# Prompt attention of a hybrid decoder: the causal mask as a GpSimd select on the weights, and plain copies of the turned weights on ScalarE or VectorE

## The chip, the cores and the metric

The kernel runs on one core of one Trainium2 chip. Its time is the device time of one execution in microseconds (us); the median over the runs is compared. The engines are called as in the profile: PE (TensorE matmul), PEld (TensorE weight load), DVE (VectorE), ACT (ScalarE), POOL (GpSimd), SP (SyncE, which issues DMAs).

## What is computed

One mixer layer of a decoder for a prompt of 2048 tokens and for 8 samples of 4 tokens: a projection into head groups (convolution, pooling, stick-breaking attention, cross-attention), gates, an output projection and norms. The change is in the stick-breaking attention of the prompt, 8 heads of 64:

```python
def sb_block(q, k, v, bias, q_pos, k_pos):
    z = (jnp.einsum('nqhd,nkhd->nhqk', q, k).astype(jnp.float32) * (SB_HEAD_DIM ** -0.5)
         + bias.astype(jnp.float32)[None, :, None, None])
    mask = (k_pos[None, :] < q_pos[:, None])[None, None]
    log_beta = jax.nn.log_sigmoid(z)
    log_1m = jnp.where(mask, jax.nn.log_sigmoid(-z), 0.0)
    rc = lax.cumsum(log_1m, axis=3, reverse=True)
    a = jnp.exp(jnp.where(mask, log_beta + rc - log_1m, -jnp.inf))
    return jnp.einsum('nhqk,nkhd->nqhd', a.astype(v.dtype), v)
```

For each query the weight of key k is beta(k), the sigmoid of the score, times the product of (1 - beta) over all later keys before the query. Keys from the query's own position on have weight zero.

## The kernel before

The program has three stages in a row: the projection with the sample group's attention beside it (to about 1476 us of the profile), the prompt's attention (to about 1946 us), and the output projection. All operations are handed to a scheduler that sets the order on ACT, DVE, POOL and SP; on PE the order is the one in which the code issues them (`manual_schedule`, L145). Every engine works through its own queue in order.

`sb_prompt` (L1289) goes over 16 blocks: head pair `hp` 0 to 3, and in each the query block `qb` 0 to 3 of 512 queries. In a block the key chunks `kc` of 512 keys run from `qb` down to 0; the chunk `kc == qb` is the diagonal one (`dg`). Each chunk has four steps, one for head `hh` 0 or 1 and `q2` 0 or 2, a pair of query tiles of 128 rows. So a head pair has 40 steps, 16 of them diagonal, and the stage has 160.

One step, in `score`:
- PE computes the scores S of two query tiles against `w` keys (512, or 256 in the diagonal chunk's first pair; L1267, two buffers).
- ACT makes the gates from S: `gam` = 1 - beta (L1271, three buffers in turn) and the weight factor `be` = beta (L1272).
- `rest`, which is issued two steps later, has DVE scan `gam` backwards into the running product E (L1337 in a diagonal chunk, L1340 in others, one scan per tile; the scan's second operand ZM is a mask column in PSUM that starts the diagonal products), and POOL multiply `be` by E in place (L1349, one product per tile) and keep E's last column in `cr` as the next chunk's start (L1345).

Six steps after a chunk's first step, `turn` takes its 128-key squares: for key tile `r` and head `hh` PE transposes the up to four squares into one PSUM tile AT (L1360, two buffers), which is taken out to `at` in SBUF (four buffers). In a diagonal chunk the squares before tile r are skipped, so the tile has 512, 384, 256 or 128 columns, and the exit is a product with the triangle `tri` on DVE (L1364): it clears the entries of keys that do not come before the query. In other chunks it is a copy on ACT (L1366). Two steps after that `values` multiplies `at` with the values into the accumulator `av` (L1376, a single buffer), and at a block's end DVE multiplies `av` with the gate into `sbo` (L1381).

The first two steps (head pair 0, block 0, `q2` 0) are computed ahead by `sb_early` (L1274) into a buffer named `early`, while the projection still runs. `zm` and `tri` are built on POOL at the start of the stage (L1293 to L1300); ACT copies `zm` into PSUM as ZM (L1297).

Between the steps a side task is stepped: the end of the sample group's attention (nS, nE, nyn, nys: L1076 to L1137), sums of output weights on POOL (`ws`, L1587), splits of weights (ACT L1623, POOL L1628) and of activations (ACT L1717, POOL L1728), and the start of the convolution's tail (cs, cm, L1447 to L1459).

## Time and profile before

| | |
|---|---|
| median of 3 runs | 2351.18 us |
| the three runs | 2357.12, 2351.18, 2350.86 us |
| span of the profiled execution | 2357.7 us |
| DVE, ACT, POOL busy over the span | 1705.4, 1115.4, 1299.0 us |
| the stage with the prompt's attention | about 1476 to 1946 us |

The profile is of one execution, whose span is 6.5 us above the median of the timed runs; for its own time only this span is given. A row of a group or a tile reads: line, engine, operation, output <- inputs, shape and count, then busy time and mean, or minimum, median and maximum in ns. A row of the timeline starts with the start time and the length in us, and has the idle time of the engine ahead of it, and what ended that, in square brackets. "PE AT L1360 <- DVE at L1364" in the waits view reads: on PE, the instruction of line 1360 that writes AT waited for the one of line 1364 on DVE that writes `at`.

### The profile page before, as it was taken

How to read it: one execution, taken by the hardware profiler on the slowest of the kernel's cores; microseconds unless marked ns; L12 is line 12 of the kernel's file. 1: busy time of each engine (PE TensorE's matmuls, PEld its weight loads, DVE VectorE, ACT ScalarE, POOL GpSimd, SP SyncE). 2: the span in 40 equal slices, each digit the busy share in tenths (PEclk: the TensorE clock that was granted, in tenths of full speed). 3: DMA queues.
4: the chain of work that ended last, by engine and by line, in shares of the span. 5: the costliest groups of instructions: out<-in, count | busy, mean ns of one | idle time of the engine just before them, and what ended most of it. 6: DMA issues, size and time to landing. Idle time of an engine off the chain costs nothing. (4 is left out here: it accounts for less than half of the span.)

```text
span 2357.7 us, 42145 instructions
## 1 busy us (share of the span) xinstructions
PE 2270.5 (96%) x16000; PEld 1762.9 (75%) x16000; DVE 1705.4 (72%) x2372; ACT 1115.4 (47%) x1935; POOL 1299.0 (55%) x1347
## 2 busy tenths in 40 slices
PE   7999999999999999999999999899999999999997
PEld 7898888888888777777777777555555557788775
DVE  5342786969657673577787868988897966586997
ACT  5332342242442322224242324798989875453553
POOL 3554546555565546545546463688988854432333
PEclk9999999999999999999999999999999999999999
DMA  6689987878678899987877785656544207876764
GB/s 208 199 293 308 332 273 255 278 254 290 240 260 314 314 350 341 321 286 257 304 264 258 274 269 148 178 166 167 163 124 117 77 23 231 277 230 190 244 244 145
DMA packets 336868, 557.94 MB, mean 237 GB/s; under 512 B 27985, under 2 KB 212433, under 8 KB 320266
## 3 DMA queue, kind: packets, MB, share of 16 engines
q1 hardware_dynamic: 281290, 286.53, 39.3%
q0 software_dynamic: 55376, 268.72, 32.0%
q8 instruction: 126, 2.06, 0.3%
q14 instruction: 76, 0.62, 0.1%
HBM read 465.09 MB, written 90.68 MB: 236 GB/s over the span
## 5 line engine op out<-in xcount | busy, mean ns | idle before, releaser
L971 DVE STREAM_TRANSPOSE T<-kt 128x1024 f32<-128x1024 f32 x256 | 308.7, 1226 | 188.7 <-PE sSA L984 176.3
L938 POOL DMA_INDIRECT vt<-in_cache_v_dram,idv x256 | 253.2, 989 | 256.1 <-PE sO L1023 195.3
L623 DVE SCALAR_TENSOR_TENSOR cacc<-U,par,cacc 128x512 f32<-128x512 f32 x480 | 359.9, 750 | 11.0
L1349 POOL TENSOR_TENSOR be<-be,E 128x512 f32<-128x512 f32 (+3 forms) x316 | 300.3, 965 | 59.6 <-DVE E L1340 26.7
L1340 DVE TENSOR_TENSOR_SCAN E<-gam,cr,ZM 128x513 f32<-128x513 f32 x192 | 232.8, 1263 | 14.2 <-ACT gam L1271 10.8
L938 POOL DMA_INDIRECT kt<-in_cache_k_dram,idk x128 | 127.7, 998 | 196.4 <-DVE T L971 151.3
L1360 PEld LDWEIGHTS AT<-ident,be 128*128 128x128 f32 x1082 | 115.7, 141 | 130.0 <-ACT at L1366 48.3
L1993 PE MATMUL acc<-wohi,mh 128*128 128x512 f32 (+1 forms) x480 | 194.2, 405 | 1.2 <-ACT mh L1717 1.2
L1271 ACT ACTIVATE gam<-S,nbias_bc 128x1024 f32<-128x1024 f32 (+1 forms) x158 | 173.1, 1096 | 42.4 <-ACT be L1272 19.4
L1993 PE MATMUL acc<-wolo,mh 128*128 128x512 f32 (+1 forms) x480 | 190.4, 397 | 0.7 <-DVE wolo L1628 0.7
L1993 PE MATMUL acc<-wohi,ml 128*128 128x512 f32 x448 | 178.6, 399 | 8.0 <-DVE ml L1728 8.0
L1267 PE MATMUL S<-kT,Q 128*128 128x512 f32 (+1 forms) x632 | 173.6, 397 | 4.3 <-ACT be L1272 4.3
L1272 ACT ACTIVATE be<-S,bias_bc 128x1024 f32<-128x1024 f32 (+1 forms) x158 | 172.1, 1089 | 0.8 <-DMA gsd<-sg1sg 0.8
L1360 PE MATMUL AT<-ident,be 128*128 128x128 f32 x1082 | 157.0, 282 | 15.7 <-DVE at L1364 8.6
L1376 PE MATMUL av<-at,V 128*64 128x512 f32 (+3 forms) x640 | 151.9, 554 | 3.5 <-DVE sbo L1381 3.5
L984 PE MATMUL sSA<-T,W 128*32 128x128 f32 x4096 | 140.0, 276 | 2.8 <-DVE T L971 1.4
L984 PEld LDWEIGHTS sSA<-T,W 128*32 128x32 f32 x4096 | 105.3, 109 | 38.7 <-issue 31.9
L1728 DVE TENSOR_TENSOR ml<-mr,mh 128x512 fp32r<-128x512 f32 x108 | 93.2, 869 | 45.2 <-ACT mh L1717 43.5
L1023 PE MATMUL sO<-vt,saT 128*32 128x512 f32 x1024 | 122.4, 592 | 0.0
L1267 PEld LDWEIGHTS S<-kT,Q 128*128 128x128 f32 x632 | 104.3, 192 | 18.1 <-ACT be L1272 5.8
L1366 ACT COPY at<-AT 128x512 f32<-128x512 f32 x192 | 111.3, 680 | 12.2 <-PE AT L1360 12.2
L1337 DVE TENSOR_TENSOR_SCAN E<-gam,ZM 128x384 f32<-128x384 f32 (+1 forms) x124 | 94.3, 811 | 28.8 <-ACT gam L1271 21.9
(584 smaller groups left out, 6021.5 us busy)
## 6 DMA issues: line engine op xcount, KB each, us to landing
Q<-qd SPq DMA_DIRECT2D x64, 256.0 KB
mr<-mixd SPq DMA_DIRECT2D x32, 512.0 KB
mr<-mixd SPq DMA_DIRECT2D x48, 256.0 KB
xtp<-in_x_prompt_dram SPq DMA_DIRECT2D x16, 512.0 KB
kT<-kd SPq DMA_DIRECT2D x64, 128.0 KB
ws<-in_w_out_dram SPq DMA_DIRECT2D x16, 512.0 KB
wsd<-ws SPq DMA_DIRECT2D x16, 512.0 KB
msd<-mr SPq DMA_DIRECT2D x32, 256.0 KB
```

Of the source, the lines that this page charges most:

```text
L623: dve.scalar_tensor_tensor(out=ps, in0=U[:, a + k : a + k + H], scalar=wd[:, k : k + 1], in1=ps, op0=ALU.mult, op1=ALU.add)
L938: pool.indirect_dma_start(out=dst, out_offset=None, in_=rows, in_offset=bass.IndirectOffsetOnAxis(ap=idx, axis=0))
L971: S["turn"] = dve.transpose(T[:, 2 * hh : 2 * hh + 2].rearrange("p s j t -> p (s j t)"), kt[:, 2 * hh : 2 * hh + 2].rearrange("p s j d -> ...
L984: pe.matmul(sSs[n][32 * g : 32 * g + 32, P * ml : P * (ml + 1)], lhsT=W[:, jj, :], rhs=T[:, :, jj, :], start=i == 0, stop=i == 3, tile_pos ...
L1267: pe.matmul(S[:, j, :w], lhsT=Q[:, x, P * (q2 + j) : P * (q2 + j + 1)], rhs=kt[:, :w], start=x == 0, stop=x == 1)
L1271: act.activation(out=ga, in_=S[:, :, :w], func=AF.Sigmoid, bias=nbias_bc[:, h : h + 1], scale=-1.0)
L1272: act.activation(out=be, in_=S[:, :, :w], func=AF.Sigmoid, bias=bias_bc[:, h : h + 1])
L1340: dve.tensor_tensor_scan(out=E[:, j][:, ::-1], data0=g_[:, j][:, ::-1], data1=ZM[:, 0:1].to_broadcast([P, 513]), initial=carry[hh, q2][:, ...
L1349: newest.append(pool.tensor_tensor(out=be[:, j, :m], in0=be[:, j, :m], in1=E[:, j, 513 - w : 513 - w + m], op=ALU.mult).ins)
L1360: pe.transpose(ap_[:, P * qt : P * (qt + 1)], A[hp, qb, kc, hh, qt][:, P * r : P * (r + 1)], ident)
L1376: pe.matmul(av[64 * hh : 64 * hh + 64, c], lhsT=V[:, 4 * kc + r, 64 * hh : 64 * hh + 64], rhs=ats.pop((hp, qb, kc, r, hh))[:, c], start=dg ...
L1993: pe.matmul(o[:rows], lhsT=m[a][:, k, :rows], rhs=W[prod, 4 * h + k][w], start=not cont and h == k == n == 0, stop=h == 1 and k == 3 and n ...
```

## The change

The triangle `tri` is gone. A new function `sb_shut` clears, right behind the gates of a diagonal step, the two 128 x 128 squares of `be` that lie on the diagonal, with one select on POOL (`affine_select` over 2 x 128 columns, in place); POOL's products follow on the cleared tile. The early steps get the same, on the buffer `early`. So the turned squares need no mask, and each of the 320 exits from PSUM is a plain copy, on ACT or on DVE. Which one is decided when the program is built: `spent` adds up an estimate of the work that each of the two has got lately (gates and copies for ACT, scans and copies for DVE), the copy goes to the engine that would be done first, and an engine may fall at most SLACK = 3 us behind the other in that account.

```diff
--- before.py
+++ after.py
@@ -62,6 +62,7 @@
 MSTEP = 5
 KT = 2
 WR = 2
+SLACK = 3.0
 
 
 class Tasks:
@@ -1271,6 +1272,13 @@
         act.activation(out=ga, in_=S[:, :, :w], func=AF.Sigmoid, bias=nbias_bc[:, h : h + 1], scale=-1.0)
         act.activation(out=be, in_=S[:, :, :w], func=AF.Sigmoid, bias=bias_bc[:, h : h + 1])
 
+    def sb_shut(be, q2):
+
+        two = be[:, 0, P * q2 : P * q2 + P]
+        two = bass.AP(tensor=two.tensor, offset=two.offset, ap=[two.ap[0], [be.ap[1][0] + P, 2], [1, P]])
+        pool.affine_select(out=two, in_=two, compare_op=ALU.is_gt, fill=0.0, base=0, pattern=[[0, 2], [-1, P]],
+                           channel_multiplier=1)
+
     def sb_early(load, blk, sbr, bps, early):
 
         room = sbr.tile([P, 16, P], F32, tag="V", name="early", bufs=2).rearrange("p (n j b) c -> p n j (b c)", n=4, j=2)
@@ -1284,6 +1292,7 @@
             sb_scores(S, hh, 0, 2 * P, Q[hh], KT[0, hh, 0])
             early[hh] = room[:, 2 * hh], room[:, 2 * hh + 1]
             sb_gates(S, hh, 2 * P, *early[hh])
+            sb_shut(early[hh][1], 0)
             yield
 
     def sb_prompt(load, loaded, sb, bps, ops, zmp, early, values_of, flags, newest):
@@ -1295,10 +1304,6 @@
                            pattern=[[-1, P]], channel_multiplier=1)
         ZM = zmp.tile([P, 512], F32, name="ZM", bufs=1)
         act.copy(ZM, zm)
-        tri = sb.tile([P, 512], F32, name="tri", bufs=1)
-        pool.memset(tri, 1.0)
-        pool.affine_select(out=tri, in_=tri, compare_op=ALU.is_gt, fill=0.0, base=0, pattern=[[1, 512]],
-                           channel_multiplier=-1)
         gam = []
         for k in range(3):
             g = sb.tile([P, 2, 513], F32, name=f"gam{k}", bufs=1)
@@ -1307,6 +1312,12 @@
         blocks = [(hp, qb) for hp in range(4) for qb in range(4)]
         A, avs, ats = {}, {}, {}
         count = {"pair": 0}
+        spent = {act: 0.0, dve: 0.0}
+
+        def spend(eng, us):
+            spent[eng] += us
+            other = dve if eng is act else act
+            spent[other] = max(spent[other], spent[eng] - SLACK)
 
         def score(hp, qb, kc, hh, q2, Q, KT, carry):
 
@@ -1320,16 +1331,20 @@
             else:
                 S = ops.tile([P, 2, 512], F32, tag="S", name=f"S{nm}", bufs=2)
                 sb_scores(S, h, q2, w, Q[hh], KT[hp, hh, kc])
+                spend(act, 2 * (0.15 + 0.00166 * w))
                 be = sb.tile([P, 2, 512], F32, tag="be", name=f"be{nm}", bufs=10)
                 g_ = gam[count["pair"] % 3]
                 count["pair"] += 1
                 ga = g_[:, :, 512 - w : 512]
                 sb_gates(S, h, w, ga, be[:, :, :w])
+                if dg:
+                    sb_shut(be, q2)
             for j in range(2):
                 A[hp, qb, kc, hh, q2 + j] = be[:, j]
 
             def rest():
                 E = sb.tile([P, 2, 513], F32, tag="E", name=f"E{nm}", bufs=3)
+                spend(dve, 0.3 + 0.00204 * sum(ns))
                 for j, n in enumerate(ns):
                     if dg:
 
@@ -1360,10 +1375,14 @@
                 pe.transpose(ap_[:, P * qt : P * (qt + 1)], A[hp, qb, kc, hh, qt][:, P * r : P * (r + 1)], ident)
             at = sb.tile([P, 512], F32, tag="at", name=f"at{nm}", bufs=4)
             c = slice(P * q0, 512)
-            if dg:
-                dve.tensor_tensor(out=at[:, c], in0=ap_[:, c], in1=tri[:, : 512 - P * q0], op=ALU.mult)
+            n = 512 - P * q0
+            mine, its = 0.045 + 0.00083 * n, 0.13 + 0.00104 * n
+            if spent[act] + mine <= spent[dve] + its:
+                act.copy(at[:, c], ap_[:, c])
+                spend(act, mine)
             else:
-                act.copy(at[:, c], ap_[:, c])
+                dve.tensor_copy(at[:, c], ap_[:, c])
+                spend(dve, its)
             ats[hp, qb, kc, r, hh] = at
 
         def values(hp, qb, kc, r, V, gt):
```

The instructions on PE are the same, in the same order. On the others, as the program is built (the rows of now bear the changed kernel's line numbers, 1 to 19 higher; scans are listed as SCALAR_TENSOR_TENSOR):

ACT, at the start of the stage. S and gam are the scores and gates of the stage's first full step, ZM the mask column in PSUM. Before:

```order
L713 ACTIVATE sg1sg_1_14828<-z1sg_1_14794 128x512
L1271 ACTIVATE gam_14875<-S_0_0_0_2_14885,nbias_bc 128x2x512
L1272 ACTIVATE be_0_0_0_2_14890<-S_0_0_0_2_14885,bias_bc 128x1024
L1297 COPY ZM<-zm 128x512
L1271 ACTIVATE gam_14877<-S_0_0_1_2_14898,nbias_bc 128x2x512
L1272 ACTIVATE be_0_0_1_2_14903<-S_0_0_1_2_14898,bias_bc 128x1024
```

Now:

```order
L714 ACTIVATE sg1sg_1_14830<-z1sg_1_14795 128x512
L1272 ACTIVATE gam_14874<-S_0_0_0_2_14884,nbias_bc 128x2x512
L1306 COPY ZM<-zm 128x512
L1273 ACTIVATE be_0_0_0_2_14889<-S_0_0_0_2_14884,bias_bc 128x1024
L1272 ACTIVATE gam_14876<-S_0_0_1_2_14898,nbias_bc 128x2x512
L1273 ACTIVATE be_0_0_1_2_14903<-S_0_0_1_2_14898,bias_bc 128x1024
```

The copy of zm has moved ahead of the gate be of the first step. POOL at the same place; qz, nM, nga and nrst are set-ups for the sample group's last keys, pr is a part of the cross-attention. Before:

```order
L527 TENSOR_SCALAR pr_3_512_256_14594<-pr_3_512_256_14594,sm_3_512_256_14595 128x256 x2
L1068 MEMSET qz 128x256
L1082 MEMSET nM 32x32
L1098 MEMSET nga 32x8
L1099 MEMSET nrst 32x8x32
L1070 COPY qz<-qsT 64x4x32 x2
L1083 AFFINE_SELECT nM<-nM 32x32
L1100 MEMSET nrst 32x8
L1085 AFFINE_SELECT nM<-nM 32x32
L1087 AFFINE_SELECT nM<-nM 32x32
L1293 MEMSET zm 128x512
L1299 MEMSET tri 128x512
```

Now:

```order
L528 TENSOR_SCALAR pr_3_512_256_14594<-pr_3_512_256_14594,sm_3_512_256_14595 128x256 x2
L1279 AFFINE_SELECT early<-early 128x2x128 x2
L1069 MEMSET qz 128x256
L1083 MEMSET nM 32x32
L1099 MEMSET nga 32x8
L1100 MEMSET nrst 32x8x32
L1071 COPY qz<-qsT 64x4x32 x2
L1084 AFFINE_SELECT nM<-nM 32x32
L1101 MEMSET nrst 32x8
L1086 AFFINE_SELECT nM<-nM 32x32
L1088 AFFINE_SELECT nM<-nM 32x32
L1302 MEMSET zm 128x512
```

The two early selects (x2) stand ahead of the set-ups and of zm; three small fills of gam and the select of zm follow next.

DVE, head pair 1, where block 1 follows block 0. The head pair is not in these names: E_1_0_0_2 is the scan of qb 1, kc 0, head 0, q2 2, and at_0_0_2_1 the exit of qb 0, kc 0, r 2, head 1. Before:

```order
L1337 SCALAR_TENSOR_TENSOR E_1_1_1_2_16394<-gam_14875,ZM 128x384
L1337 SCALAR_TENSOR_TENSOR E_1_1_1_2_16394<-gam_14875,ZM 128x512
L1364 TENSOR_TENSOR at_0_0_2_0_16379<-AT_0_0_2_0_16376,tri 128x256
L1364 TENSOR_TENSOR at_0_0_2_1_16384<-AT_0_0_2_1_16381,tri 128x256
L1340 SCALAR_TENSOR_TENSOR E_1_0_0_0_16420<-gam_14877,cr_1_1_0_0_16305,ZM 128x513 x2
L1364 TENSOR_TENSOR at_0_0_3_0_16406<-AT_0_0_3_0_16404,tri 128x128
L1364 TENSOR_TENSOR at_0_0_3_1_16410<-AT_0_0_3_1_16408,tri 128x128
L1340 SCALAR_TENSOR_TENSOR E_1_0_0_2_16450<-gam_14879,cr_1_1_0_2_16336,ZM 128x513 x2
L1364 TENSOR_TENSOR at_1_1_0_0_16432<-AT_1_1_0_0_16427,tri 128x512
L1364 TENSOR_TENSOR at_1_1_0_1_16439<-AT_1_1_0_1_16434,tri 128x512
L1381 TENSOR_TENSOR sbo_0_16457<-av_0_16373,sgt_0_16097 128x512
L1364 TENSOR_TENSOR at_1_1_1_0_16464<-AT_1_1_1_0_16460,tri 128x384
```

Now:

```order
L1352 SCALAR_TENSOR_TENSOR E_1_1_1_2_16415<-gam_14874,ZM 128x512
L1355 SCALAR_TENSOR_TENSOR E_1_0_0_0_16441<-gam_14876,cr_1_1_0_0_16325,ZM 128x513
L1384 COPY at_0_0_2_0_16400<-AT_0_0_2_0_16397 128x256
L1384 COPY at_0_0_2_1_16405<-AT_0_0_2_1_16402 128x256
L1355 SCALAR_TENSOR_TENSOR E_1_0_0_0_16441<-gam_14876,cr_1_1_0_0_16325,ZM 128x513
L1355 SCALAR_TENSOR_TENSOR E_1_0_0_2_16471<-gam_14878,cr_1_1_0_2_16357,ZM 128x513 x2
L1384 COPY at_0_0_3_1_16431<-AT_0_0_3_1_16429 128x128
L1355 SCALAR_TENSOR_TENSOR E_1_0_1_0_16516<-gam_14874,cr_1_1_1_0_16390,ZM 128x513 x2
L1400 TENSOR_TENSOR sbo_0_16478<-av_0_16394,sgt_0_16110 128x512
L1355 SCALAR_TENSOR_TENSOR E_1_0_1_2_16544<-gam_14876,cr_1_1_1_2_16418,ZM 128x513 x2
L1384 COPY at_1_1_1_1_16491<-AT_1_1_1_1_16487 128x384
```

In these rows DVE had seven exits of turned tiles and now has four, one of them from further down; the others are on ACT. The whole program has 86 copies on DVE (66 of 512 columns, 8 of 384, 8 of 256, 4 of 128) and 234 on ACT (158, 24, 24, 28).

POOL, head pair 0, a diagonal chunk (qb 2, kc 2). Before:

```order
L1349 TENSOR_TENSOR be_2_2_0_0_15196<-be_2_2_0_0_15196,E_2_2_0_0_15248 128x127
L1345 COPY cr_2_2_0_0_15251<-E_2_2_0_0_15248 128x2
L1349 TENSOR_TENSOR be_2_2_0_0_15196<-be_2_2_0_0_15196,E_2_2_0_0_15248 128x255
L1349 TENSOR_TENSOR be_2_2_0_2_15222<-be_2_2_0_2_15222,E_2_2_0_2_15279 128x383
L1345 COPY cr_2_2_0_2_15282<-E_2_2_0_2_15279 128x2
L1349 TENSOR_TENSOR be_2_2_0_2_15222<-be_2_2_0_2_15222,E_2_2_0_2_15279 128x511
```

Now:

```order
L1279 AFFINE_SELECT be_2_2_0_0_15201<-be_2_2_0_0_15201 128x2x128
L1360 COPY cr_2_2_0_0_15259<-E_2_2_0_0_15256 128x2
L1364 TENSOR_TENSOR be_2_2_0_0_15201<-be_2_2_0_0_15201,E_2_2_0_0_15256 128x127
L1364 TENSOR_TENSOR be_2_2_0_0_15201<-be_2_2_0_0_15201,E_2_2_0_0_15256 128x255
L1279 AFFINE_SELECT be_2_2_0_2_15228<-be_2_2_0_2_15228 128x2x128
L1360 COPY cr_2_2_0_2_15291<-E_2_2_0_2_15288 128x2
L1364 TENSOR_TENSOR be_2_2_0_2_15228<-be_2_2_0_2_15228,E_2_2_0_2_15288 128x383
L1364 TENSOR_TENSOR be_2_2_0_2_15228<-be_2_2_0_2_15228,E_2_2_0_2_15288 128x511
```

One select stands ahead of each step's two products.

## The prediction

> **What bounds the kernel now.** Two rows first, the cores view and the first table of the page.
>
> ```profile
> core 0: 2357.7 us, clock 0.994
> ```
>
> ```profile
> PE 2270.5 (96%) x16000; PEld 1762.9 (75%) x16000; DVE 1705.4 (72%) x2372; ACT 1115.4 (47%) x1935; POOL 1299.0 (55%) x1347
> ```
>
> TensorE is busy for 96% of the span, so a change that leaves its instructions alone can only take out the rest of it. The change touches the attention stage alone, 1476 to 1946 us. The windows view of it, in the columns window, length, PE, PEld, DVE, ACT, POOL busy (count), granted clock, DMA share and GB/s:
>
> ```profile
> 1480.00:1516.00 36.00, 26.59 (x145) 16.60 (x146) 34.15 (x54) 25.73 (x32) 23.03 (x33) 0.91 0.69 167
> 1640.00:1680.00 40.00, 39.30 (x216) 22.24 (x215) 36.00 (x44) 36.41 (x47) 35.21 (x43) 1.00 0.49 144
> 1720.00:1760.00 40.00, 37.75 (x212) 21.76 (x209) 38.64 (x52) 34.42 (x41) 34.90 (x43) 1.00 0.44 127
> 1480.00:1920.00 440.00, 413.95 (x2310) 241.74 (x2310) 389.06 (x484) 393.16 (x512) 366.48 (x464) 0.99 0.47 130
> ```
>
> The last row is nearly the whole stage: PE 414 of 440 us, so 26 us of idle is all there is to win. The second row is a stretch of long blocks, where PE is busy for 39.3 of 40 us; the first and the third are the starts of head pairs 0 and 2, where DVE is the fuller engine (34.15 of 36, 38.64 of 40) and PE waits. The PE queue's own waits in the stage, as total, times, longest:
>
> ```profile
> PE AT L1360 <- DVE at L1364: 8.6, 11, 1.2
> PE S L1267 <- ACT be L1272: 4.3, 2, 3.0
> PE AT L1360 <- ACT at L1366: 4.3, 12, 0.9
> PE av L1376 <- DVE sbo L1381: 3.5, 8, 1.9
> PE cm L1452 <- ACT at L1366: 1.7, 1, 1.7
> PE nS L1076 <- DVE at L1364: 1.6, 1, 1.6
> PE nys L1133 <- DVE at L1364: 1.4, 1, 1.4
> PE AT L1360 <- POOL be L1349: 0.7, 2, 0.5
> ```
>
> Together 26.1 us. The masked products on DVE (L1364) end 8.6 + 1.6 + 1.4 = 11.6 us of it. One such wait in the timeline, where the diagonal squares of one block meet the long scans of the next:
>
> ```profile
> 1735.37 0.47 DVE L1364 TENSOR_TENSOR at<-AT,tri 128x128 f32<-128x128 f32 x2
> 1735.58 0.69 ACT L1271 ACTIVATE gam<-S,nbias_bc 128x512 f32<-128x512 f32 x1 [0.89 <-DVE E L1340]
> 1735.75 0.42 DVE L1337 TENSOR_TENSOR_SCAN E<-gam,ZM 128x128 f32<-128x128 f32 x1
> 1735.76 0.31 PEld L1360 LDWEIGHTS AT<-ident,be 128*128 128x128 f32 x3 [1.56 <-POOL be L1349]
> 1735.79 0.41 PE L1360 MATMUL AT<-ident,be 128*128 128x128 f32 x2 [1.13 <-DVE at L1364]
> ```
>
> DVE goes from one piece of work to the next without a gap, ACT has just stood idle for 0.89 us because a scan was late, and PE stood for 1.13 us because its transposed squares were not yet taken out of PSUM.
>
> **The change part by part.** *Copies.* What the two kinds of copy cost now (count, minimum/median/maximum in ns; for L1364 the minimum is the 128-column form and the maximum the 512-column one):
>
> ```profile
> L1366 ACT COPY at<-AT x192: 580/647/1022, 1514.4 to 1944.0; 128x512 f32<-128x512 f32 x192
> L1364 DVE TENSOR_TENSOR at<-AT,tri x128: 252/476/692, 1488.9 to 1902.4; 128x512 f32<-128x512 f32 x32, 128x384 f32<-128x384 f32 x32, 128x256 f32<-128x256 f32 x32, 128x128 f32<-128x128 f32 x32
> ```
>
> Along the straight line from 252 to 692 ns, 384 columns cost 545 and 256 cost 399, so the 128 products are 32 x (692 + 545 + 399 + 252) = 60.4 us. Their place is taken by 320 plain copies: by the new order 86 on DVE (66 of 512 columns, 8, 8 and 4 of 384, 256 and 128) and 234 on ACT (158, 24, 24, 28). No plain DVE copy of 512 columns out of PSUM is in the trace; the nearest, of 256, is
>
> ```profile
> L443 DVE COPY mnat<-mt x8: 410/424/426, 60.6 to 115.5; 128x256 f32<-128x256 f32 x8
> ```
>
> 0.424 us beside the product's 0.399: dropping the second operand saves nothing, and I use the product's line for both. DVE then has 66 x 0.692 + 8 x 0.545 + 8 x 0.399 + 4 x 0.252 = 54.3 us, 6.1 less. For ACT's short copies:
>
> ```profile
> L382 ACT COPY nat0v<-nt0v x12: 373/479/483, 167.2 to 228.9; 128x384 f32<-128x384 f32 x8, 128x256 f32<-128x256 f32 x4
> ```
>
> 0.479 for 384, 0.373 for 256 and, along the same line, 0.267 for 128. ACT loses 34 x 0.647 = 22.0 us and gets 24 x 0.479 + 24 x 0.373 + 28 x 0.267 = 27.9: 5.9 more. So the sums hardly move; what moves is the place. Where a block of one square row is followed by a block of two, DVE had 16 products, 4 x 1.888 = 7.6 us. In the second head pair six copies stay there (512, 384, 256, 256, 128, 384 columns: 2.8 us), so DVE is 4.7 us earlier at a spot where PE waits for one to two us. The first pair keeps 3.0 us, its sixth copy having 512 columns; the third and the fourth keep 2.8. That lies on the path. I take 9.5 of the 11.6 us back and leave a fifth, because the copies that stay still stand between scans; the ends are 4 (ACT late in DVE's stead) and 11.6. Of the 3.5 us for the output product (L1381, in the same DVE queue) I take back most of the one long wait, 1.5; the short ones come from the single accumulator buffer and stay. The 4.3 us for ACT's copies lie in long blocks, where DVE now takes about one copy in four: I take half, 2.2; ends 0 and 4.3, or 4.3 more if ACT's extra copies queue behind its gates. They are hidden by ACT's own idle time, as the 0.89 above; without that cover they are 5.9 us.
>
> *Selects.* GpSimd gets 64, of 2 x 128 columns each, two of them at the start. None of that form is in the trace. The stage's opening on POOL has the nearest on either side:
>
> ```profile
> L1300 POOL TENSOR_SCALAR_AFFINE_SELECT tri<-tri 128x512 f32<-128x512 f32 x1 | 0.6, 614 | 0.0
> L1299 POOL MEMSET tri<- 128x512 f32 x1 | 0.5, 543 | 0.0
> L1293 POOL MEMSET zm<- 128x512 f32 x1 | 0.5, 532 | 20.0 <-PE z1sg L247 20.0
> L1294 POOL TENSOR_SCALAR_AFFINE_SELECT zm<-zm 128x128 f32<-128x128 f32 x1 | 0.3, 306 | 0.0
> L1305 POOL MEMSET gam<- 128x2 f32 x3 | 0.2, 92 | 0.0
> ```
>
> 306 ns for 128 columns and 614 for 512 make 0.41 for 256, which I take. The dearest select anywhere in the program, by its tile's rows, is
>
> ```profile
> L885 POOL TENSOR_SCALAR_AFFINE_SELECT e<-e x1: 925/925/925, 123.1 to 123.1; 8x128 f32<-8x128 f32 x1
> ```
>
> so the ends are 0.31 and 0.93; a price below nothing is out, since the product on POOL that follows is not shortened. 62 x 0.41 = 25.4 us against 440 - 366 = 74 us of POOL idle in the stage. Each select stands ahead of its own pair's products and behind the earlier pairs', and waits for the second gate, for which they waited too; so nothing else is held behind it. It delays them only where the scan is already done. The PEld waits tell how often POOL is last:
>
> ```profile
> PEld AT L1360 <- POOL be L1349: 23.1, 30, 1.7
> ```
>
> 30 times, yet PE itself lost 0.7 us by it, since the value products were still running. I take 1.5 us; ends 0 and what the rival below gives.
>
> The Trainium skill's page "Perfetto Trace Analysis", section "Optimizing Scalar/DVE Operations", speaks against this move: GpSimd and VectorE share an SBUF read port, so moving work between those two might not help. By it the 25.4 us would stand in DVE's way as well. In this trace DVE's 389 and POOL's 366 us fit into 440 us, so at least 315 us of them ran side by side, which does not fit an exclusion of the present scans and products.
>
> *The start.* The two early selects stand on POOL ahead of ten small set-ups and of the mask column zm (tri's two set-ups, 0.54 and 0.61 us, are gone), and the copy of zm (L1297) now stands on ACT ahead of the first gate be of the stage. POOL did the set-ups long before:
>
> ```profile
> 1454.49 0.31 POOL L1068 MEMSET qz<- 128x256 f32 x1
> ...
> 1456.44 0.26 POOL L1087 TENSOR_SCALAR_AFFINE_SELECT nM<-nM 32x32 f32<-32x32 f32 x1
> ```
>
> 2.2 us from the first start to the last end. ACT at the opening, and PE's first wait:
>
> ```profile
> 1478.54 0.71 ACT L1272 ACTIVATE early<-Se,bias_bc 128x512 f32<-128x512 f32 x1
> 1479.11 0.62 ACT L713 ACTIVATE sg1sg<-z1sg 128x512 f32<-128x512 f32 x1
> 1479.58 1.15 ACT L1271 ACTIVATE gam<-S,nbias_bc 128x1024 f32<-128x1024 f32 x1
> 1480.58 1.16 ACT L1272 ACTIVATE be<-S,bias_bc 128x1024 f32<-128x1024 f32 x1
> 1481.58 0.65 ACT L1297 COPY ZM<-zm 128x512 f32<-128x512 f32 x1
> ```
>
> ```profile
> 1481.79 1.22 PE L1267 MATMUL S<-kT,Q 128*128 128x256 f32 x4 [3.03 <-ACT be L1272]
> ```
>
> The second early gate ends at 1479.25, its select at 1479.66, the set-ups at 1481.87, zm (0.53 + 0.3 for three small fills + 0.31) at about 1483.0. ACT's copy starts then instead of at 1481.58, 1.4 us later, and the gate be behind it at 1483.5 instead of 1480.58, for which PE waits to free a score buffer. The scans shift by the 1.4, the scores by the 2.9. I take 1.8 us, near the scans' shift since DVE is the fuller engine there; ends 0 (taken up by the lighter DVE queue) and 2.9.
>
> Sum: - 9.5 - 1.5 - 2.2 + 1.5 + 1.8 = - 9.9 us. The profiled span of 2357.7 us would become 2347.8. It lies 6.5 us above the median of the three timed runs, 2351.2, from which the forecast is counted: 2341.3 us. A measurement of this kernel can tell about 0.3%, 7 us: faster begins below 2344.1, slower above 2358.2.
>
> **The rivals.** *The wait changes its name.* ACT is at 393 of 440 us, as full as DVE. If its diagonal copies queue behind two gates of 1.15 us, PE waits for ACT where it waited for DVE: only 4.6 of the 11.6 us come back and none of ACT's 4.3. - 4.6 - 1.5 + 1.5 + 1.8 = - 2.8: 2348.4. For it speaks that ACT is in front in long blocks; against it, its idle time just where DVE is full.
>
> *The shared port.* A select cannot run beside a scan. At the start of a pair four selects per block, eight in two, hold DVE for 8 x 0.41 = 3.3 of the 4.7 us won, so 1.4 / 4.7 of the 11.6, 3.5 us, come back: - 3.5 - 2.2 + 1.5 + 1.8 = - 2.4, 2348.8. Against it stands the overlap of 315 us. This is what the Trainium skill's page "Perfetto Trace Analysis" says above, taken as a mechanism.
>
> *POOL becomes the bound: slower.* The select is put into the chain gate, select, product, transpose, and POOL is the last to release the transposes 30 times already. If the cover of the value products is used up there, each pays a whole select: 30 x 0.41 = 12.3 us instead of 1.5, 2352.1; at 0.93 us 27.9, 2367.7. It decides from (2358.2 - 2341.3 + 1.5) / 30 = 0.61 us per such place. For it speaks the row 1640 to 1680, where POOL has 35.21 of 40 us; against it the 0.7 us.
>
> *More than forecast.* If the better balance takes all of the 26.1 us but the first scores' 4.3, cm's 1.7 and 2.0 of the output product's: - 18.1 + 1.8 = - 16.3, 2334.9.
>
> That the change doesn't take place is no rival: the new order has the selects and the copies, with PE's instructions as before.
>
> **How the numbers follow.** Forecast 0.45 (its own range 2336 to 2346, 0.40 of it faster and 0.05 the same), changed name 0.28, shared port 0.05, POOL 0.12, more 0.10. Faster 0.40 + 0.10 = 0.50, same 0.05 + 0.28 + 0.05 = 0.38, slower 0.12. The range of 2333 to 2354 takes in the case of more and both even ones, and leaves out the greater part of POOL's.
>
> **What would show it.** Right: the PE waits for DVE at gone to about 2 us, ACT's near 2, POOL's below 2.5; selects of 0.3 to 0.5 us; the first score wait about 2 us longer; PE in 1720 to 1760 near 39 of 40 us. Wrong: PE waits for POOL be of 10 us or more, selects over 0.6 us, or ACT at above 8 us.

## The result, and the profile after

The changed kernel is slower. Its median is 2366.19 us over ten runs (2360.70 to 2376.95), that of the kernel before over ten runs beside them 2354.39 us (2350.86 to 2358.86); the ratio is 1.0048, with a 95% interval of 1.0032 to 1.0064. A second measurement (changed_again, below) gave 2367.08 to 2354.44 us, 1.0064 (1.0042 to 1.0087). The forecast was 2341.3 us, and the range ended at 2354.

First the length of the stage, since single runs of one kernel lie up to 16 us apart in these measurements and up to 19 in later ones. I measure it from the start of the first early gate on ACT to the start of the last output product `sbo` on DVE. For the kernel before, a row of the timeline and one of the tile sbo (minimum, median and maximum in ns, first and last start):

```profile
1476.82 0.69 ACT L1271 ACTIVATE early<-Se,nbias_bc 128x512 f32<-128x512 f32 x1
...
L1381 DVE TENSOR_TENSOR sbo<-av,sgt x16: 652/667/692, 1506.1 to 1946.5; 128x512 f32<-128x512 f32 x16
```

The same two rows of the changed kernel:

```profile
1476.01 0.69 ACT L1272 ACTIVATE early<-Se,nbias_bc 128x512 f32<-128x512 f32 x1
...
L1400 DVE TENSOR_TENSOR sbo<-av,sgt x16: 662/681/692, 1505.8 to 1959.5; 128x512 f32<-128x512 f32 x16
```

Before, the stage takes 1946.5 - 1476.8 = 469.7 us, now 1959.5 - 1476.0 = 483.5: 13.8 us more, where the medians differ by 11.8. The windows view over the whole stage (columns as in the prediction), before and after, with the same 2448 matmuls in both:

```profile
1476.80:1946.50 469.70, 441.47 (x2448) 258.30 (x2447) 393.82 (x489) 408.16 (x539) 373.90 (x477) 0.99 0.45 126
1476.00:1959.50 483.50, 445.44 (x2448) 259.91 (x2447) 390.86 (x448) 416.20 (x581) 399.06 (x549) 0.98 0.45 122
```

PE stands idle for 38.1 us instead of 28.2, and is busy for 4.0 us longer with the same work at a lower granted clock (the last section). The windows of the prediction, for the changed kernel; they are the same times, but no longer quite the same work, since the stage falls behind:

```profile
1480.00:1516.00 36.00, 27.55 (x156) 18.40 (x156) 31.55 (x44) 29.57 (x43) 30.38 (x57) 0.86 0.71 144
1640.00:1680.00 40.00, 38.32 (x211) 21.88 (x210) 35.15 (x38) 35.78 (x49) 36.64 (x48) 1.00 0.40 112
1720.00:1760.00 40.00, 38.41 (x216) 22.23 (x215) 35.06 (x44) 36.16 (x50) 36.11 (x55) 1.00 0.41 115
1480.00:1920.00 440.00, 406.53 (x2252) 236.97 (x2252) 373.24 (x426) 390.58 (x540) 381.94 (x525) 0.98 0.48 130
```

In 440 us PE was busy for 406.5 us instead of 414.0, and DVE stood idle for 67 us instead of 51. ACT, the fullest of the others, has 390.6 us where it had 393.2, and over the whole stage 86% where it had 87%. So no engine became the bound; PE and DVE wait more. The PE queue's own waits in the stage (all of them add up to 37.6 us, 26.5 before):

```profile
PE AT L1375 <- DVE at L1384: 20.2, 19, 4.3
PE AT L1375 <- ACT at L1381: 6.4, 13, 1.9
PE S L1268 <- ACT be L1273: 6.4, 2, 5.6
PE nS L1077 <- DVE at L1384: 1.1, 1, 1.1
PE AT L1375 <- POOL be L1364: 1.0, 1, 1.0
PE av L1395 <- DVE sbo L1400: 1.0, 1, 1.0
```

The wait that the change was to remove, PE for DVE's copies, has grown from 8.6 to 20.2 us, though fewer copies stand on DVE. What else has grown is seen on ACT and DVE. Three rows of the waits of before, from ACT's and DVE's queues:

```profile
ACT at L1366 <- PE AT L1360: 12.2, 6, 3.1
ACT gam L1271 <- PE S L1267: 1.6, 4, 0.8
DVE E L1337 <- ACT gam L1271: 21.9, 17, 2.1
```

and the same three after:

```profile
ACT at L1381 <- PE AT L1375: 31.0, 34, 4.7
ACT gam L1272 <- PE S L1268: 22.1, 57, 1.6
DVE E L1352 <- ACT gam L1272: 35.7, 29, 2.1
```

ACT now stands at copies whose squares PE has not turned (34 times, not 6), its gates come late for scores that PE has not computed (57 times, not 4), and DVE's scans come late for the gates. ACT as a whole is hardly more idle (49.4 of the 440 us, 46.8 before); but before, its gates waited 12.5 us for DVE's scans, and now they wait for none. I read this as the engines having fallen into step with PE. The timeline of the changed kernel at the end of the first block of head pair 1 shows how:

```profile
1620.22 3.62 DVE L1355 TENSOR_TENSOR_SCAN E<-gam,cr,ZM 128x513 f32<-128x513 f32 x3
...
1621.67 0.26 ACT L1381 COPY at<-AT 128x128 f32<-128x128 f32 x1
...
1623.76 0.27 DVE L1384 COPY at<-AT 128x128 f32<-128x128 f32 x1
1623.81 0.61 ACT L1381 COPY at<-AT 128x512 f32<-128x512 f32 x1
...
1624.17 0.63 PE L1375 MATMUL AT<-ident,be 128*128 128x128 f32 x4 [1.34 <-DVE at L1384]
...
1624.84 0.59 ACT L1381 COPY at<-AT 128x512 f32<-128x512 f32 x1 [0.41 <-PE AT L1375]
```

The two heads' tiles of one turn have been given to two engines. ACT takes its tile out at once; the other, a copy of 0.27 us, stands in DVE's queue behind three scans of 1.2 us. PE has only two AT buffers, so it waits 1.34 us for that small copy, and then ACT waits for PE. By the queues of the built program it happens in every second turn: of the stage's 160 turns, 78 are split over the two engines, 4 are on DVE and 78 on ACT. Before, none was split (64 on DVE, 96 on ACT).

One large wait lies elsewhere. The timeline at 1513 to 1523 us:

```profile
1513.36 0.38 SPq L1117 DMA_DIRECT2D ngc<-gnd  x1
...
1519.01 0.48 DVE L1121 TENSOR_SCALAR nrb<-ident,ngc 128x128 f32<-128x128 f32 x2 [5.30 <-DMA ngc<-gnd]
...
1522.10 1.12 PE L1375 MATMUL AT<-ident,be 128*128 128x128 f32 x4 [4.27 <-DVE at L1384]
...
1522.87 2.06 PE L1268 MATMUL S<-kT,Q 128*128 128x512 f32 x4
```

`nrb` belongs to the side task of the sample group and needs a column that goes through DRAM. In the kernel before that transfer was issued at 1509.5 us and DVE came to nrb at 1515.1 without a wait. Now DVE, with fewer copies, came to it 1.4 us earlier, and the transfer was issued 3.9 us later, since the chain ahead of it came later (the scan nE on DVE at 1501.9 instead of 1499.9 us, the copy ngt on POOL, behind a product, at 1503.4 instead of 1500.7, then eight stores on SP).

What the forecast had right of the rows:

```profile
L1279 POOL TENSOR_SCALAR_AFFINE_SELECT be<-be 128x256 f32<-128x256 f32 x62 | 25.2, 406 | 14.0 <-ACT be L1273 14.0
...
L1384 DVE COPY at<-AT x86: 266/666/693, 1489.4 to 1952.8; 128x512 f32<-128x512 f32 x66, 128x384 f32<-128x384 f32 x8, 128x256 f32<-128x256 f32 x8, 128x128 f32<-128x128 f32 x4
```

A select takes 0.41 us, as estimated, and a copy out of PSUM 0.27 to 0.69 us on DVE, as priced.

### The profile page after: what moved, and what is told of

The parts are those of the page before. It is cut to its first block, busy times and chain, and to the rows that moved or that the text cites. A ratio compares the mean times of both kernels' runs of the same rounds, so it can differ in the third digit from the quotient of the medians.

```text
span 2365.0 us, 42227 instructions
## 1 busy us (share of the span) xinstructions
PE 2269.3 (96%) x16000; PEld 1762.1 (75%) x16000; DVE 1701.2 (72%) x2330; ACT 1123.3 (47%) x1977; POOL 1318.5 (56%) x1409
## 3 DMA queue, kind: packets, MB, share of 16 engines
q8 instruction: 126, 2.06, 0.4%
## 5 line engine op out<-in xcount | busy, mean ns | idle before, releaser
L1355 DVE TENSOR_TENSOR_SCAN E<-gam,cr,ZM 128x513 f32<-128x513 f32 x192 | 234.0, 1266 | 11.6 <-ACT gam L1272 9.8
L1375 PE MATMUL AT<-ident,be 128*128 128x128 f32 x1082 | 161.6, 285 | 28.1 <-DVE at L1384 20.2
L1272 ACT ACTIVATE gam<-S,nbias_bc 128x1024 f32<-128x1024 f32 (+1 forms) x158 | 167.7, 1061 | 29.0 <-PE S L1268 22.1
L1273 ACT ACTIVATE be<-S,bias_bc 128x1024 f32<-128x1024 f32 (+1 forms) x158 | 166.5, 1054 | 0.0
L1381 ACT COPY at<-AT 128x512 f32<-128x512 f32 (+3 forms) x234 | 117.6, 541 | 31.5 <-PE AT L1375 31.0
```

The costliest lines, as they stand in the source:

```text
L1272: act.activation(out=ga, in_=S[:, :, :w], func=AF.Sigmoid, bias=nbias_bc[:, h : h + 1], scale=-1.0)
L1273: act.activation(out=be, in_=S[:, :, :w], func=AF.Sigmoid, bias=bias_bc[:, h : h + 1])
L1355: dve.tensor_tensor_scan(out=E[:, j][:, ::-1], data0=g_[:, j][:, ::-1], data1=ZM[:, 0:1].to_broadcast([P, 513]), initial=carry[hh, q2][:, ...
L1375: pe.transpose(ap_[:, P * qt : P * (qt + 1)], A[hp, qb, kc, hh, qt][:, P * r : P * (r + 1)], ident)
```

## The experiments

Each run below is timed beside runs of the kernel before on the same chip. The table gives medians, the ratio with its 95% interval, and from the run's one profile the length of the stage, measured as above, with two parts of it: from the first gate to the first gate of block 3 of head pair 0 (start), and from there to that of the last chunk (rest).

| run | us | before, us | ratio | stage | start | rest |
|---|---|---|---|---|---|---|
| kernel before (first profile) | | | | 469.7 | 68.1 | 363.0 |
| before_again | 2357.45 | 2356.63 | 1.0004 (0.9989 to 1.0018) | 469.5 | 68.1 | 362.8 |
| changed kernel | 2366.19 | 2354.39 | 1.0048 (1.0032 to 1.0064) | 483.5 | 72.3 | 371.8 |
| changed_again | 2367.08 | 2354.44 | 1.0064 (1.0042 to 1.0087) | 480.3 | 68.3 | 372.7 |
| nrb_later | 2364.59 | 2355.52 | 1.0038 (1.0021 to 1.0055) | 478.0 | 67.1 | 371.5 |
| nrb_later_no_select | 2363.22 | 2355.52 | 1.0034 (1.0019 to 1.0050) | 476.8 | 65.7 | 371.7 |
| nrb_later_early_after | 2363.85 | 2355.52 | 1.0035 (1.0018 to 1.0051) | 476.7 | 65.8 | 371.5 |
| nrb_later_old_split | 2359.51 | 2355.52 | 1.0020 (1.0006 to 1.0033) | 473.0 | 70.5 | 363.9 |
| old_split_all_fixed | 2358.89 | 2354.44 | 1.0016 (1.0005 to 1.0027) | 474.5 | 72.1 | 363.7 |
| only_diagonals_shared | 2362.13 | 2354.44 | 1.0034 (1.0022 to 1.0046) | 481.2 | 67.1 | 375.7 |
| diagonals_one_each | 2368.58 | 2354.44 | 1.0053 (1.0038 to 1.0068) | 481.6 | 68.9 | 374.3 |
| copies_ahead_of_scans | 2358.90 | 2358.06 | 0.9996 (0.9981 to 1.0012) | 475.8 | 71.3 | 366.1 |
| one_each_copies_ahead | 2368.37 | 2358.06 | 1.0041 (1.0026 to 1.0057) | 480.1 | 68.7 | 372.2 |
| old_split_copies_ahead | 2380.89 | 2358.06 | 1.0093 (1.0077 to 1.0109) | 489.0 | 68.5 | 381.1 |
| selects_twice | 2369.56 | 2358.06 | 1.0057 (1.0040 to 1.0075) | 482.6 | 71.4 | 371.8 |
| sample_product_ahead | 2348.45 | 2356.63 | 0.9970 (0.9954 to 0.9985) | 469.0 | 66.0 | 364.8 |
| first_blocks_only | 2355.71 | 2356.63 | 1.0007 (0.9990 to 1.0024) | 470.1 | 64.5 | 366.9 |
| pairs_together | 2347.72 | 2356.63 | 0.9970 (0.9956 to 0.9983) | 465.0 | 65.9 | 360.9 |
| pairs_only | 2349.56 | 2356.29 | 0.9982 (0.9966 to 0.9997) | 465.8 | 68.2 | 359.3 |
| pairs_copies_ahead | 2354.98 | 2356.29 | 0.9995 (0.9982 to 1.0009) | 468.8 | 65.4 | 364.1 |

### The wait for the sample column

nrb_later builds `nrb` behind the side task's six pauses and ties it to the latest scan, so that it stands six places later in DVE's queue:

```diff
-        rbs = []
-        for k in range(2): ... nrb ...
         for _ in range(6):
             yield
+        rbs = []
+        for k in range(2):
+            rb = sm.tile([P, P], F32, tag="nrb", name=f"nrb{k}", bufs=2)
+            with tc.issue_after(scans[-1]):
+                dve.tensor_scalar(out=rb, in0=ident, scalar1=gc[:, k : k + 1], scalar2=None, op0=ALU.mult)
+            rbs.append(rb)
```

> The changed kernel with one edit: VectorE's two small products nrb (the identity times the column ngc that a DMA brings) stand six places later in VectorE's queue, every other instruction of every engine where it was. Theory A (the loss is mostly one wait: VectorE reaches nrb 5.3 us before its transfer, PE stands 4.27 us behind it and then runs at half clock): VectorE no longer waits for ngc, the granted clock of 1516 to 1560 goes from 0.92 to 1.00, and the time falls by about 7 us, from 2366 to 2359. Theory B (the loss is spread: copies that stand behind scans or gates in their queues all through the stage, and the next late thing takes the place of this wait): 2364 to 2366.

The wait is gone, and the stage is 5.5 us shorter than in the changed kernel's first profile. But the median fell by 2 us only, within the intervals. So the changed kernel was profiled again, as it is:

> The changed kernel as it is, a second profile and a second measure beside the runs of this group. If the 5.3 us wait of VectorE for the column ngc belongs to the order of the queues, it is there again with 4 to 6 us, and the attention stage is as long as in the first profile within 1 us. If it hangs on how the transfers happen to fall, it is below 3 us here, which would explain why moving nrb gained 2 us in the median and not the 6 us that the stage of its profile lost.

Its row of the same wait:

```profile
DVE nrb L1121 <- DMA ngc<-gnd: 2.5, 1, 2.5
```

Half as long, and the stage 480.3 us: this wait hangs on how transfers fall in an execution. Theory A is wrong in the main: the wait is real, and worth 2.3 us (480.3 - 478.0) to 5.5 us. The other 8.3 us of the loss (478.0 - 469.7) lie elsewhere. The kernel before, profiled again, shows that its stage doesn't move like that:

> The kernel before, profiled a second time. If the order of its queues fixes the stage, its length is 469.7 us as in the first profile within 1 us, and the differences of the other profiles to it are those of the kernels. If transfers move it as they moved the changed kernel's (483.5 and 480.3 us), it is off by 3 us or more.

469.5 beside 469.7 us: the stage of this kernel is steady. That of the changed kernel is not, 483.5 and 480.3 us, and nearly all of this lies in the start (72.3 and 68.3; the rest 371.8 and 372.7). So a difference of some us in the rest belongs to the kernels, while one in the start, which rests on one profile each, can belong to the execution.

### The selects and the start

nrb_later_no_select leaves both calls of the select out, so the diagonal squares stay unmasked:

```diff
-            sb_shut(early[hh][1], 0)
...
-                if dg:
-                    sb_shut(be, q2)
```

> The changed kernel with nrb later and without any of the 64 selects; the diagonal squares stay unmasked, and the queues of all engines but GpSimd are instruction by instruction those of nrb_later. Theories A and B: the selects stand in GpSimd's idle time except for the two early ones, so 1 to 3 us less than nrb_later, and that by the start alone. The rival of the prediction, POOL as the bound: 12 us or more less.

nrb_later_early_after moves only the early ones, behind their products in `rest`:

```diff
-            sb_shut(early[hh][1], 0)
...
+                if (hp, qb, q2) == (0, 0, 0):
+                    sb_shut(be, 0)
```

> The changed kernel with nrb later and the two early selects put behind their products, so that GpSimd's set-ups and the mask column zm are done before the gates as in the kernel before; nothing else moves. If the start costs what it delays: PE's first score wait falls from 5.6 to about 3.0 us and the time by 1.5 to 2.6 us against nrb_later. If a later wait takes the start's delay up (the first blocks' scans are the fuller work): within 1 us of nrb_later.

Both shorten the stage by the same: 478.0 to 476.8 and to 476.7. So in these profiles the early selects cost 1.3 us through the start, and the other 62 nothing that shows; the medians, about 1 us apart, can't tell. selects_twice calls the select twice in each diagonal step:

```diff
                 if dg:
                     sb_shut(be, q2)
+                    sb_shut(be, q2)
```

> As nrb_later, with each of the 62 selects of the stage's own pairs done twice, the second time on squares already cleared; the other engines' queues have the same order. If POOL's chain bounds as the prediction's slower rival has it: 62 times 0.41 us of more work on POOL, about 30 of them on the path, 12 us slower. If the selects stand in idle time: within 2 us of nrb_later.

The rest of the stage, 371.8 us, is that of nrb_later (371.5) with 25 us more on POOL. The start took about 4 us more: one wait of PE for DVE's copies grew from 2.34 to 4.15 us, and PE ran at half clock for 6.8 us behind it instead of 3.4. So with this division POOL has room for one select everywhere, and for a second everywhere but in the opening. POOL as the bound is refuted.

### The division of the copies

nrb_later_old_split and old_split_all_fixed keep the selects and plain copies, and divide them as before; the second has the start mended as well:

```diff
-            if spent[act] + mine <= spent[dve] + its:
+            if not dg:
```

> The changed kernel with nrb later and the copies divided as in the kernel before (the diagonal ones all on VectorE, as plain copies, the others all on ScalarE); the 64 selects stay. Theory A: nothing but the start is left of the loss, so as nrb_later, 2358 to 2360. Theory B: the new division is what costs, so this is 4 to 8 us faster than nrb_later and within 2 us of the kernel before. If the selects cost (POOL as the bound): 2364 or more.

> Selects kept, nrb later, early selects behind their products, and the copies divided as before (diagonal ones on VectorE, others on ScalarE). If start and division are all that is left of the loss: within 2 us of the kernel before, and the stage within 1.5 us of its stage. If the plain copies and selects have a gain of their own over the masked products: 2 us or more faster than the kernel before; the forecast's theory had none.

The rest falls from 371.5 to 363.9 and 363.7 us, within 1 us of the kernel before. So it is the division that costs 8 us there, and the mask's move by itself neither gains nor loses there. In the start the old division is the worse, 70.5 us against 67.1 in nrb_later: there the account may relieve DVE, but part of the 3.4 us is a longer stretch of PE at half clock (the last section), which old_split_all_fixed has too. Its start of 72.1 us is why its stage, 474.5 us, missed its expectation.

Which copies do the harm? Theory C had the long ones off the diagonal:

```diff
-            if spent[act] + mine <= spent[dve] + its:
+            if not dg or spent[act] + mine <= spent[dve] + its:
```

> nrb later, early selects behind their products; copies of rows off the diagonal all on ScalarE as before, only the diagonal ones are given out by the account (43 on VectorE, 85 on ScalarE). Theory C (the long copies off the diagonal, which the account gives to VectorE, are what makes PE wait, since each stands between the long scans of VectorE's queue; 6.8 us of the 16.5 us in the profile of nrb_later): the waits of PE for VectorE's copies fall from 16.4 to about 9 us, and the time is 4 to 7 us below that of nrb_later_early_after. Rival D (ScalarE, with 85 copies more and some 427 of 440 us busy, becomes the bound): PE's waits for ScalarE's copies go from 6 to over 12 us and the time does not fall.

```diff
-            if spent[act] + mine <= spent[dve] + its:
+            if not dg or hh == 0:
```

> As only_diagonals_shared, but without an account: of each pair of diagonal copies the first head's is on ScalarE and the second's on VectorE (64 each). Theory C: waits of PE for VectorE's copies 4 to 8 us, the time at or below that of the kernel before, by up to 5 us. Rival D in its milder form (ScalarE some 420 of 440 us): ScalarE's waits rise by as much, the time as old_split_all_fixed or slower.

Theory C fell with both. With no long copy off the diagonal on DVE, the PE waits for it were 16.3 and 18.3 us. The second is the plainest case: it is the old division, except that of each pair of diagonal copies one went to ACT. In the window of 440 us DVE had 30 us less to do than in old_split_all_fixed and ACT 11 more, and the rest took 374.3 us instead of 363.7. Rival D, ACT's load, fails too: PE's waits for ACT's copies were 7.0 and 4.2 us, and pairs_together below has the same 400 of 440 us on ACT as diagonals_one_each (400.4 and 400.8) without the loss.

The bare number of split turns does not set the loss either. By the account of the program only_diagonals_shared splits 29 turns, where the change splits 78, and PE's waits in its stage add up to 31.7 us, as in nrb_later_early_after. Its rest is 4.2 us longer than there, of which half clock can make most: behind three waits of 1.98 us PE ran at it for 3.4 us each.

### Place or pair

Two explanations were left: a copy's place behind long scans (theory F), or that a turn waits for two queues (theory H). copies_ahead_of_scans ties the scans behind the copies that the program issues before them:

```diff
+                  with tc.issue_after(outs[-1]) if outs else ExitStack():
                     ... the scans of a step ...
-                dve.tensor_copy(at[:, c], ap_[:, c])
+                outs.append(dve.tensor_copy(at[:, c], ap_[:, c]).ins)
```

> As nrb_later_early_after, with the division of the change, and one edit: in VectorE's queue a copy stands ahead of the scans that the program issues after it (the order of the program), where the build's order let up to three of those long scans go first. Theory F (what PE waits for is the place of a copy behind long scans, not VectorE's load): PE's waits for VectorE's copies fall from 16.4 to below 7 us, and the time by 5 to 9 us against nrb_later_early_after, to the kernel before or a little below it. Rival G (VectorE then stands at copies whose transposes PE has not done, its scans come later, and PE waits for products or score buffers instead): the sum of PE's waits in the stage stays within 4 us, and so does the time.

The rest fell from 371.5 to 366.1 us and the waits for DVE's copies from 16.4 to 1.7, as theory F had it. But PE's waits for POOL's products rose from 1.4 to 6.8 us, and the start took 5.5 us more. Its timeline there:

```profile
1538.98 7.13 DVE L1356 TENSOR_TENSOR_SCAN E<-gam,cr,ZM 128x513 f32<-128x513 f32 x6
...
1541.13 0.65 PE L1135 MATMUL nys<-nrb,Oc 128*64 128x128 f32 x4 [0.36 <-ACT at L1385]
...
1546.04 1.53 DVE L1139 TENSOR_TENSOR nym<-nys,nyns 64x32 f32<-64x32 f32 x8
...
1547.72 0.45 PE L1379 MATMUL AT<-ident,be 128*128 128x128 f32 x1 [3.75 <-DVE nym L1139]
```

`nys` lies in one of the two AT buffers, and its readers stood behind six scans. sample_product_ahead adds them to the copies that go first:

```diff
-            dve.tensor_tensor(out=ym[...], in0=yb[...], in1=yn[:, h], op=ALU.add)
+            outs.append(dve.tensor_tensor(out=ym[...], in0=yb[...], in1=yn[:, h], op=ALU.add).ins)
```

> As copies_ahead_of_scans, and one instruction group moved: the eight small products nym stand four long scans earlier in VectorE's queue. Their operand nys lies in one of the two PSUM buffers of the turns, so until they are done only one buffer turns. If that is what the first blocks lost (PE waited 3.8 us once and ran at half clock after it): the first six chunks take 66 to 67 us instead of 71.3, and the stage 471 instead of 475.8. If not, both stay.

The start took 66.0 us, as expected, and the stage 469.0, two less than expected. The medians of these two runs lie 5.2 and 7.5 us lower than their stages say (with stages 6.1 us longer and 0.7 shorter than before, they are 0.8 us above and 8.2 below the kernel before). In the other runs the two agree within 5 us. The profile of copies_ahead_of_scans is of its slowest execution, 2369.5 us where the fastest took 2350.2; in that of sample_product_ahead the part behind the stage took 400.1 us, and 402 to 411 in every other run. Whether these explain it stays open: a profile is one execution, and the median is of several.

The same order on two other divisions:

> As diagonals_one_each (of each pair of diagonal copies one on ScalarE, one on VectorE), with the copies ahead of the later scans in VectorE's queue. Theory F: PE's waits for VectorE's copies fall from 18.3 to below 8 us, and the time by 6 to 10 us against diagonals_one_each. Rival G: they fall, but others rise by as much.

> As old_split_all_fixed (diagonal copies on VectorE in pairs, the others on ScalarE), with the copies ahead of the later scans. Theory F: its 8.9 us of waits for VectorE's copies fall to 4 to 6 us and the time by 3 to 5 us. Rival G: no change in the time, as above.

The first gained 1.5 us of stage, and the second lost 14.5. So "copies first" is no cure by itself. In one_each_copies_ahead PE's waits for DVE's copies fell from 18.3 to 1.6 us, but others rose, those for POOL's products from 0.8 us and those for the output product from none that shows:

```profile
PE AT L1379 <- POOL be L1366: 6.9, 14, 0.8
...
PE av L1399 <- DVE sbo L1404: 6.0, 4, 1.9
```

That is rival G. DVE's waits for PE's transposes in old_split_all_fixed:

```profile
DVE at L1387 <- PE AT L1378: 6.8, 8, 1.7
```

and in old_split_copies_ahead:

```profile
DVE at L1388 <- PE AT L1379: 43.8, 13, 4.9
```

With copies first, DVE stands at copies that are not ready, and the scans behind them come late: rival G again, and more than that, where the copies come in pairs on DVE.

Theory H was then tested by itself. pairs_together asks the account once per turn, with start and nrb mended; pairs_only makes the same edit on the changed kernel and no other:

```diff
+        pick = [True]
...
-            if spent[act] + mine <= spent[dve] + its:
+            if hh == 0:
+                pick[0] = spent[act] + mine <= spent[dve] + its
+            if pick[0]:
```

> As nrb_later_early_after, but the account is asked once per turn, and both heads' copies go to the engine that it names (86 copies on VectorE, 234 on ScalarE as before, in pairs). Theory H (a turn whose two copies stand in two queues waits for the later of both engines): PE's waits for copies, 16.4 and 6.0 us, fall to about 8 and 6, and the stage, 476.7 us there, to 469 to 472. Theory F (the place behind long scans): as many long copies stand on VectorE and as far behind scans, so the stage stays at 475 us or longer.

> The changed kernel with one edit: the account is asked once per turn, and both heads' copies go to the engine it names. The early selects and nrb stand where the change has them. Theory H (the split pairs are the main cost): the start's 2 us and 0 to 4 us of the wait for the column ngc stay, the rest goes as in pairs_together; stage 467 to 471 us against 480.3 and 483.5, time 10 to 17 us below the changed kernel, 0 to 5 us below the kernel before. If the three causes are of like size: 473 us or more.

With as many copies on each engine as in the change (86 and 234), but no turn split, the stage takes 465.0 and 465.8 us, and the medians are below the kernel before. The edit also moves copies: by the account 92 of the 320 stand on the other engine than in the change, and DVE has 60, 18, 8 and 0 of the four sizes instead of 66, 8, 8 and 4. At the prediction's prices this is the same work on DVE, 54.5 us and 54.2. PE's waits in the stage of pairs_only:

```profile
PE AT L1376 <- ACT at L1384: 7.2, 14, 1.9
PE S L1268 <- ACT be L1273: 6.4, 2, 5.6
PE av L1398 <- DVE sbo L1403: 5.9, 7, 1.2
...
PE AT L1376 <- DVE at L1387: 0.6, 1, 0.6
```

The waits for DVE's copies are nearly gone, and with them the lockstep. ACT's waits of the same run:

```profile
ACT at L1384 <- PE AT L1376: 13.3, 11, 3.1
...
ACT gam L1272 <- PE S L1268: 2.2, 5, 0.5
```

31.0 and 22.1 us have become 13.3 and 2.2. The place in the timeline that was shown for the changed kernel looks like this in pairs_only:

```profile
1619.64 3.81 DVE L1353 TENSOR_TENSOR_SCAN E<-gam,ZM 128x128 f32<-128x128 f32 x6
...
1621.12 0.43 ACT L1384 COPY at<-AT 128x128 f32<-128x128 f32 x2
...
1621.53 1.07 PE L1376 MATMUL AT<-ident,be 128*128 128x128 f32 x8 [0.23 <-ACT at L1384]
```

DVE runs its scans without a stop, both small copies are on ACT, and PE waits 0.23 us. DVE's wait for the sample column was still there (2.7 us), and PE lost 0.73 us there. The start is 68.2 us, 2.4 us longer than in pairs_together, where this wait and the early selects' delay are mended.

> As sample_product_ahead (copies ahead of the later scans, nym early), with the pairs kept together. If place and split are one cost seen from two sides: nothing is left to gain, the stage 465 to 469 us. If VectorE's waiting for transposes decides, as it did in old_split_copies_ahead with pairs in the program's order: the stage 472 us or more. If the two add: 461 us or less.

Both cures together, 468.8 us, are no better than either (465.0 and 469.0). This fits one cost seen from two sides: a split turn hurts where one of its copies stands behind scans. It does not prove it, since putting copies ahead has a cost of its own. Keeping the pairs together helped in the changed kernel and in the mended one; putting the copies ahead helped with the account's division, and hardly or not at all with the two others.

Last, first_blocks_only used the new division in the first three blocks and the old one behind them:

```diff
-            if spent[act] + mine <= spent[dve] + its:
+            if spent[act] + mine <= spent[dve] + its if (hp, qb) < (0, 3) else not dg:
```

> The best parts of the profiles put together: selects with the early ones behind their products, nrb later, the new division in the first three blocks of the first head pair and the old one (diagonal copies on VectorE, others on ScalarE) behind them. If the parts add up: first six chunks 66 us as in nrb_later_early_after, the rest 364 as in old_split_all_fixed, the stage about 468 to 469 us, 1 to 2 us below the kernel before, which the times cannot tell from no change. If the division's gain there was only borrowed from the blocks behind: the stage 471 or more.

The start took 64.5 us, but the rest 366.9 instead of 363.7. Of the 7.6 us gained in the start against old_split_all_fixed, 4.4 are left in the stage (470.1 and 474.5): the gain seems partly borrowed. How much is not shown, since half clock moves both parts: old_split_all_fixed has 17.1 us of it in the start, first_blocks_only 6.8 there and 3.4 in the rest. The time is that of the kernel before.

## Why the prediction was wrong

*What bounds the kernel:* right. PE's idle time in the stage was all that could be won, and apart from the two runs named above the medians follow the length of the stage within 5 us.

*Copies:* this is the step that failed. The counts and durations were right: 86 and 234 copies at the prices given. "I take 9.5 of the 11.6 us back" was wrong in sign: PE's waits for DVE's copies went from 8.6 to 20.2 us (16.9 us in changed_again), and with the waits of nS and nys, as the forecast counted them, from 11.6 to 21.3. The step reasoned with sums of work, "DVE is 4.7 us earlier at a spot where PE waits", and set its lower end at 4 us of gain. It did not ask what the account does to a turn: it gives out single tiles, so 78 of 160 turns were split, and PE, with two AT buffers, waits for the later of two in-order queues. The new order of the build, which the prediction had counted through, shows this; I read from it how many copies went where and not which two belong together. That the split is what costs was shown from both sides: with the pairs kept, by one edit, the stage went from 480.3 and 483.5 to 465.8 us, and with the old division and its diagonal pairs split the rest of the stage went from 363.7 to 374.3. How far it costs by itself and how far by the place of the split copy behind scans the runs do not separate.

The 4.7 us themselves were too many. They count the diagonal copies that leave DVE at the start of a pair, and not the three of 512 columns off the diagonal that the account puts on DVE in the chunk behind them (3 x 0.692 = 2.1 us). And the sum for DVE's copies is 54.2 us, not 54.3, on which nothing hangs.

With the pairs kept the direction of the forecast comes true, and by the stage nearly half of its 9.9 us: 469.7 - 465.8 = 3.9 us, 4.7 in pairs_together; the medians are 6.7 and 8.9 us below the kernel before. DVE's copies then gave back nearly what was forecast: of 11.6 us, 2.8 are left in pairs_only (0.6 at the turns, 1.5 at nS, 0.7 at nyn). But ACT's copies went up to 7.2 us where half of 4.3 was forecast, and the output product to 5.9 where 1.5 of 3.5 was to go.

*The first head pair:* "the first pair keeps 3.0 us" of DVE's work, and a gain may show: the start takes 67.1 us by the new division against 70.5 by the old one, with nrb later in both, but PE ran at half clock for 10.2 us in the first and 13.7 in the second.

*Selects:* 0.41 us each, right; 1.5 us in the sum, too much: with and without the 62 the stage was the same within 0.1 us.

*The start:* the mechanism was right to the place. ACT's ZM waited for zm, the gate be came later, and PE's first score wait went from 3.03 to 5.6 us, as "about 2 us longer" had it; its cost was 1.3 us in the stage where 1.8 was taken, by one profile each.

*What was not on the list:* the sample group's column. The prediction looked at the copies' and selects' queues, not at a side task's small chain that runs through DVE, POOL and SP at the same place. There DVE reaches nrb earlier, and the transfer starts later. Its cost differs from execution to execution, 2.3 to 5.5 us of stage.

*The rivals:* "the wait changes its name" assumed that ACT would hold PE where DVE had; ACT's waits went up by 2 us only (4.3 to 6.4). POOL as the bound, the only slower rival, was refuted by selects_twice, so the slower result came about by a mechanism that had no chance of its own. None of the three signs of being wrong showed (PE's waits for POOL's be 1.0 us, selects 0.41 us, ACT's copies 6.4 us): DVE's waits growing was not among them. That the dearest form of that rival, 2367.7 us, lies next to the measured 2366.2 is chance: it needed selects of 0.93 us, and they took 0.41. The shared port of the Trainium skill's page "Perfetto Trace Analysis", section "Optimizing Scalar/DVE Operations", was not seen either: 25 us more of selects left the rest of the stage as it was (371.8 and 371.5 us), and the 192 long scans took 1.27 us each on average with no, one and two selects in a diagonal step.

## What to carry to other kernels

Where work is given out to two in-order queues by a running sum of costs, look first at what the consumer needs together: tiles that free the same few buffers belong in one queue, or the consumer waits for the later of the two wherever one stands behind long work, and both engines then wait for it. Equal loads say nothing about that, and the bare number of splits little (29 and 78 split turns, 31.7 us of PE's waits each); read the new order of each queue at the places where two results meet. And an engine that becomes lighter reaches everything in its queue earlier, also the small side work whose transfer has not become earlier.
